# Down projection of sixteen experts: column groups, scatter and layout of the weights

## The chip, the core and the metric

The kernel runs on one core of a Trainium2 chip. Its engines work side by side, each through its own list of instructions in order: TensorE (PE; its weight loads are listed apart as PEld), VectorE (DVE), ScalarE (ACT), GpSimd (POOL) and SyncE (SP), which here issues the loads of weights. Sixteen DMA engines move the data. The metric is the time of one execution on the device in microseconds (us), median over runs.

## The reference

Two transformer blocks run over 256 tokens of 1024 columns, in fp32. The first has a mixer (linear attention beside differential attention) and a layer of sixteen experts; the second has latent and windowed attention, each followed by an MLP. The change lies in the experts, where each expert takes the 32 tokens with the highest affinity to it:

```python
aff = softmax(h @ w_router); top_aff, top_idx = top_k(aff.T, 32)      # 16 experts, 32 tokens each
xin = h[top_idx]
g, u = xin @ w_gate, xin @ w_up                                       # [1024, 1024] per expert
y = (silu(g) * u) @ w_down * top_aff                                  # w_down [1024 (F), 1024 (D)]
f = zeros(256, 1024).at[top_idx].add(y)
x = x + gt2 * rmsnorm(f, norm_post_ffn)
```

## The kernel before

**Weights.** All large weights stream through a ring of slots of 1 MB (128 partitions of 8 KB) in the order of their use, listed in `queue_loads` (L1644 on). A slot is loaded again when the work on it is done: `ring.done` issues the next load of the list into the slot just freed, on SP's queue (L99). Several pools of slots exist. In the experts there are rings A (3 slots), B (4), C (5), D (3) and X (5, no longer refilled after expert 1); C and D are no longer refilled after expert 13 (L1792). An expert has twelve slots: four of gate and four of up alternating, then four of down. The two layers' memory weights (two slots each) come in after the experts 5 and 7.

**An expert** (`experts`, L996 on) goes through these steps.

- Gate and up (L1022): 32 tokens need 32 columns of the array only, so each quarter of F has its own group of 32 columns; four matmuls of 256 columns run for each of the eight parts of the contraction. An fp32 matmul is two instructions in the trace.
- The scatter matrix S (L1029 to L1032), [4 x 32 slots, 256 tokens]: the 32 slots four times over on the 128 partitions, with the affinity at the token's place.
- silu(g) * u on ScalarE and VectorE (L1034 to L1038), two transposes (L1041) and a copy `hs` (L1043), by which F lies on the partitions.
- Down (L1051): the slot g holds the rows 256 g to 256 g + 255 of `w_down`, in two parts c of 128 rows; row p of a part lies on partition p. The slot feeds the group g of 32 columns only, for both halves n of the columns of D, which go to two banks `pd[n]`. So a group holds the sum over a quarter of F.
- Evacuation (L1066): `pd[0]` by VectorE, `pd[1]` by ScalarE, into `yp` [128, 1024].
- Scatter (L1068): `acc[T][n] += S^T yp` for two tiles T of tokens and two halves n; the contraction over 128 partitions sums the four groups too. `acc` holds four banks over all experts.

The last expert takes its down weights by quarters of the columns instead (L1055 to L1068, the line of the matmuls is L1062), each slot on all four groups, so that a quarter is evacuated and scattered as soon as it is done.

`side[e]` adds other work behind some experts: the gathering of later experts' inputs behind experts 1 and 2, the norm, keys and values of the memory behind 4 to 9, the second gate behind 11. On TensorE some of it lies between the down matmuls of an expert.

After the last expert, `rms_add` (L246) takes for each of the four `acc[T][n]` a sum of squares on ScalarE (L251) and a product with the gate on VectorE (L252), then the factor per token and the sum into x (L259). The second block begins with transposes of x (L1156).

Of the kernel before, what the change touches and what calls it, by code (L numbers as in the profile page):

```python
# [19 lines left out]
P = 128  # L20
D = 1024
# [4 lines left out]
# ---------------------------------------------------------------- constants of shapes alone  # L26
# [49 lines left out]
class Ring:  # L76
    """Slots of [P, 2048] that the weights stream through, in the order in which they are used."""
# [8 lines left out]
    def want(self, key, src, part=0, parts=1):  # L86
        """src [P, k, n] in DRAM, or the part-th of the parts of it"""
        self.queue.append((key, src, part, parts))

    def load(self, pool):  # L90
        """the next of the queue into a slot; then the later parts of what has its slot"""
        self.n += 1
        t = pool.tile([P, 2048], F32, tag="ring", name=f"ring{self.n}")
        while True:
            key, src, part, parts = self.queue.pop(0)
# [27 lines left out]
class K:  # L123
# [14 lines left out]
    def isqrt(self, pool, a, m=1, out=None, part=P):  # L138
        """a ** -0.5 for a [P, m] tile: exp(-ln(a) / 2), then a step of Newton's."""
# [14 lines left out]
    def rstd(self, pool, ss, n, m=1, out=None, part=P):  # L154
        """(ss / n + eps) ** -0.5 for a [P, m] tile of sums of squares."""
        a = pool.tile([part, m], F32, tag="rs_a", bufs=2, name=self.nm("rs_a"))
        self.nc.vector.tensor_scalar(a, ss, 1.0 / n, EPS, op0=ALU.mult, op1=ALU.add)
        return self.isqrt(pool, a, m, out, part)

    def split(self, raw, n, view=lambda v: v, eng=None):  # L160
        """the two parts of [P, n] weights, n at most 512"""
# [7 lines left out]
    def three(self, out, a, w, a_st, first, last, asl, wsl):  # L169
        """out += a_hi w_hi + a_hi w_lo + a_lo w_hi, with a or w stationary."""  # L170
# [6 lines left out]
def ada_col(k, t, ps, pool, dst, tag, tbufs):  # L177
    """512 columns of the modulation for silu(c), silu(c_ctx): those of d = 4 p + j at dst [p, 2, j]."""
    nc = k.nc
# [15 lines left out]
def ada_quarter(k, q, ps, pool, dst):  # L195
    """256 columns of scale and of shift for silu(c), silu(c_ctx): those of d = 256 q + 2 p + j at dst [p, 2, 2, j]."""
    nc = k.nc
    pa = ps.tile([P, 2, P], F32, tag="o", bufs=1, name=k.nm("pa"))
    for i in range(2):
        rv = k.ring.get("ada4", q, i).rearrange("p k (n j) -> p k j n", j=2)  # L200
        # columns of the array by j and by half of the contraction
# [15 lines left out]
def ada_sum(k, t, h, pool, dst):  # L217
    """half the contraction of 512 columns of the modulation for silu(c), still to be summed over the partitions."""
# [9 lines left out]
def second_gate(k, st, pool, ps):  # L228
    """the gate of the second residual, in the place of the sums that it is made of"""
# [16 lines left out]
def rms_add(k, pool, acc, x, G, tmp, junk, order):  # L246
    """x += G * rmsnorm(acc), of 1024 columns; order: that in which the halves come"""
# [14 lines left out]
def first_mixer(k, perm, st, ringA):  # L262
    """x += gt1 * rmsnorm(mixer(x)); leaves the modulations of what follows in st."""
# [33 lines left out]
    # ------------------------------------------------ loads  # L297
# [31 lines left out]
    # ------------------------------------------------ silu(c), silu(c_ctx)  # L329
# [14 lines left out]
    # ------------------------------------------------ normalised, modulated inputs, transposed and split  # L344
# [17 lines left out]
    def quarter(q):  # L362
        """the rows of h @ W's contraction d = 256 q + ..."""
# [20 lines left out]
    def project(seg, tks, hks, pts):  # L384
        """a part of the contraction of one segment of the input projection."""
# [30 lines left out]
    # what is needed to the end, and what the linear attention alone needs  # L416
# [4 lines left out]
    # ------------------------------------------------ constants  # L421
# [14 lines left out]
    def constants(d):  # L436
        """what the linear attention needs in direction d."""
# [8 lines left out]
    # ------------------------------------------------ lower bound  # L446
# [17 lines left out]
    def gates(d, pts):  # L464
        """k = 1 - f and log f in two parts."""
# [24 lines left out]
    def decayed(d, tk, more=()):  # L490
        """k * exp(sum of the log f that follow within the tile, and all of those of `more`)."""
# [10 lines left out]
    def state(pairs):  # L502
        """sum of k^T v over token tiles, per head."""
# [9 lines left out]
    def transposed(dst, src, scale=1.0):  # L513
        """dst [P, 4, P] (or two [P, 2, P]) <- per head transposes of src [P, 512]."""
# [11 lines left out]
    # ------------------------------------------------ values, gates and states of the linear attention  # L526
# [3 lines left out]
    for seg, d in ((3, 0), (4, 1)):  # L530
# [8 lines left out]
        # what the first tile of the direction adds to the state that enters its second  # L539
# [11 lines left out]
    # ------------------------------------------------ linear attention  # L551
# [8 lines left out]
    def powers(u):  # L560
        """exp of sums of log f over spans of tokens, times k and q."""
# [24 lines left out]
    def scores(u):  # L586
        """scores [s, r] within a tile."""
# [48 lines left out]
    # ------------------------------------------------ lambda  # L636
# [15 lines left out]
    # ------------------------------------------------ keys of the differential attention  # L652
# [26 lines left out]
    # ------------------------------------------------ gate of the linear attention's output  # L679
# [15 lines left out]
    # ------------------------------------------------ values and queries of the differential attention  # L695
    # ------------------------------------------------ modulation ahead of the experts, gates of the residuals
# [5 lines left out]
    # the router on the rows before their norm: A2 * Wr, and B2 Wr on every partition  # L702
# [27 lines left out]
    # ------------------------------------------------ gates of the residuals  # L730
# [14 lines left out]
    # ------------------------------------------------ differential attention  # L745
# [4 lines left out]
    def weights(u):  # L750
# [10 lines left out]
        # p0 - lam (den0 / den1) p1, to be divided by den0  # L761
# [21 lines left out]
    # ------------------------------------------------ output projection and residual  # L783
    acc = []

    def turned_cat(c, tp):
        """128 columns of cat, transposed and split."""
# [1034 lines left out]
```

## Time and profile before

| | us |
|---|---|
| median of 3 runs | 1429.52 |
| lowest and highest | 1427.45, 1433.12 |
| span of the profiled execution | 1424.5 |

For the profiled execution the span alone is given, from its first to its last instruction; it lies 5.0 us under the median of the runs. The experts' matmuls begin at about 382 us and the second block at about 858 us of the span. The page divides the span into 40 slices and gives the bytes moved in each. The view of stretches gives for any stretch the busy time of each engine, the clock granted to TensorE (1.00 is 2.4 GHz, 0.50 is 1.2 GHz) and the rate of the transfers. The chain of waits goes back from the last instruction to what released each; the timeline lists the instructions in order of time, alike neighbours merged.

### The profile page before, as it was taken

The numbers are of one execution on the slowest core, as the hardware profiler recorded it, in microseconds if no ns is written. First come the engines' busy times: TensorE is split into PE (matmuls) and PEld (weight loads), VectorE is DVE, ScalarE is ACT, GpSimd is POOL, SyncE is SP. The second block draws the span as 40 slices with busy tenths as digits, with TensorE's granted clock in tenths as the row PEclk, the third lists the DMA queues.
The fourth block names the chain that finished last, engine by engine and source line by source line (L and its number), as shares of the span: only waits on it lengthen the run. The fifth ranks groups of instructions, "written<-read, shape, count | busy, mean of one in ns | idle before, by whom it ended". The sixth has DMA issues, their size and how long they took to land.

```text
span 1424.5 us, 22187 instructions
## 1 busy us (share of the span) xinstructions
PE 1309.2 (92%) x8719; PEld 927.4 (65%) x8719; DVE 711.3 (50%) x1595; ACT 574.1 (40%) x1304; POOL 147.3 (10%) x161
## 2 busy tenths in 40 slices
PE   5999988988699988999999879999999999999997
PEld 4776677855335433444433338889989888898996
DVE  5566788667511111111101017857566576766655
ACT  3466223486211112111110126646555555565554
POOL 1112443074000000000000002200000002000000
PEclk9999999999699999999999989999999999999999
DMA  9723513785799999999999994435655643356540
GB/s 317 257 89 136 190 34 83 248 317 178 312 415 391 368 417 416 395 413 397 416 415 416 418 393 147 150 95 178 199 186 199 195 140 90 107 194 201 180 161 30
DMA packets 103236, 352.10 MB, mean 247 GB/s; under 512 B 7041, under 2 KB 20002, under 8 KB 86236
## 3 DMA queue, kind: packets, MB, share of 16 engines
q1 hardware_dynamic: 101024, 346.86, 65.4%
q0 software_dynamic: 1344, 3.21, 0.9%
q8 instruction: 68, 1.11, 0.3%
q10 hardware_dynamic: 764, 0.63, 0.1%
q14 instruction: 36, 0.29, 0.1%
HBM read 349.62 MB, written 1.05 MB: 246 GB/s over the span
## 4 chain that ended last, share of the span: by engine, by line
PE 76%; DVE 11%; ACT 5%; issue 5%; DMA 3%; POOL 0%; ACTq 0%; DVEq 0%; POOLq 0%
PE pd L1051 12%; PE mpu L173 11%; PE macc L173 11%; PE pj L173 5%; PE eacc L1068 4%; PE pg L1022 4%; PE oacc L173 3%; PE pu L1022 3%; DVE wlo L166 2%; PE pk L173 2%; PE spu L173 2%; PE gp L935 2%; PE ob L1200 2%; DMA ring<-in_w_gate_dram 1%; ACT whi L165 1%
## 5 line engine op out<-in xcount | busy, mean ns | idle before, releaser
L166 DVE TENSOR_TENSOR wlo<-ring,whi 128x512 fp32r<-128x512 f32 (+3 forms) x459 | 306.6, 674 | 243.6 <-ACT whi L165 242.3
L165 ACT CAST whi<-ring 128x512 fp32r<-128x512 f32 (+3 forms) x465 | 273.0, 595 | 286.3 <-DVE wlo L166 127.4
L1051 PE MATMUL pd<-ring,hs 128*32 128x512 f32 x480 | 172.4, 631 | 6.9 <-ACT hs L1043 6.9
L173 PE MATMUL mpu<-h,whi 128*128 128x256 f32 x1024 | 177.7, 277 | 0.4 <-ACT whi L165 0.4
L173 PE MATMUL macc<-whi,a 128*128 128x512 f32 x512 | 160.9, 391 | 0.0
L173 PEld LDWEIGHTS mpu<-h,whi 128*128 128x128 f32 x1024 | 155.5, 188 | 1.3 <-ACT whi L165 0.8
L173 PE MATMUL mpu<-h,wlo 128*128 128x256 f32 x512 | 141.0, 277 | 0.6 <-DVE wlo L166 0.6
L173 PE MATMUL pj<-whi,hT 128*128 128x512 f32 x416 | 136.5, 401 | 0.0
L1051 PEld LDWEIGHTS pd<-ring,hs 128*32 128x32 f32 x480 | 41.2, 115 | 118.4 <-issue 106.4
L173 PEld LDWEIGHTS macc<-whi,a 128*128 128x128 f32 x512 | 96.2, 188 | 19.7
L173 PE MATMUL macc<-wlo,a 128*128 128x512 f32 x256 | 100.4, 392 | 0.0
L173 PEld LDWEIGHTS mpu<-h,wlo 128*128 128x128 f32 x512 | 96.2, 188 | 1.5 <-DVE wlo L166 1.0
L173 PEld LDWEIGHTS pj<-whi,hT 128*128 128x128 f32 x416 | 77.6, 188 | 17.1 <-ACT whi L165 0.2
L173 PE MATMUL pj<-wlo,hT 128*128 128x512 f32 x208 | 83.5, 402 | 0.0
L1022 PE MATMUL pg<-ring,xin 128*32 128x256 f32 x1024 | 71.8, 386 | 1.9 <-DMA ring<-in_w_gate_dram 1.9
L1022 PE MATMUL pu<-ring,xin 128*32 128x256 f32 x1024 | 69.9, 385 | 1.5 <-DMA ring<-in_w_up_dram 1.5
L1068 PE MATMUL eacc<-yp,S 128*128 128x512 f32 (+1 forms) x136 | 60.8, 588 | 9.5 <-ACT yp L1066 8.4
L1066 DVE COPY yp<-pd 128x512 f32<-128x512 f32 (+1 forms) x17 | 11.2, 660 | 107.1 <-PE pd L1051 103.8
L173 PEld LDWEIGHTS macc<-wlo,a 128*128 128x128 f32 x256 | 48.1, 188 | 10.6
L1068 PEld LDWEIGHTS eacc<-yp,S 128*128 128x128 f32 x136 | 24.9, 194 | 45.3 <-issue 21.9
L1066 ACT COPY yp<-pd 128x512 f32<-128x512 f32 (+1 forms) x17 | 9.5, 560 | 109.2 <-PE pd L1051 99.9
L575 POOL TENSOR_TENSOR kl<-ex,kT 128x512 f32<-128x512 f32 (+1 forms) x32 | 45.5, 1435 | 67.3 <-ACT ex L572 67.3
(492 smaller groups left out, 2066.8 us busy)
## 6 DMA issues: line engine op xcount, KB each, us to landing
ring<-in_w_gate_dram SPq DMA_DIRECT2D x64, 1024.0 KB, 9.0
ring<-in_w_up_dram SPq DMA_DIRECT2D x64, 1024.0 KB, 12.3
ring<-in_w_down_dram SPq DMA_DIRECT2D x64, 1024.0 KB, 13.6
ring<-in_mlp_w_up_dram SPq DMA_DIRECT2D x32, 1024.0 KB, 5.8
ring<-in_mlp_w_down_dram SPq DMA_DIRECT2D x32, 1024.0 KB, 5.0
ring<-in_w_ada_dram SPq DMA_DIRECT2D x24, 1024.0 KB, 7.8
ring<-in_w_in_dram SPq DMA_DIRECT2D x32, 512.0 KB, 4.9
ring<-in_w_o_dram SPq DMA_DIRECT2D x8, 1024.0 KB, 5.1
```

The source lines that it names most:

```text
L165: nc.scalar.copy(view(hi[:, :n]), raw)
L166: (eng or nc.vector).tensor_tensor(view(lo[:, :n]), raw, view(fl(hi[:, :n])), op=ALU.subtract)
L173: self.nc.tensor.matmul(out, lhsT=av if a_st else wv, rhs=wv if a_st else av, start=first and i == 0, stop=last and i == 2)
L575: nc.gpsimd.tensor_tensor(kl[half_][:, 0:n], ex[:, 0:n], kT[d][:, T, None, h, :].to_broadcast([P, n, P]), op=ALU.mult)
L935: nc.tensor.matmul(gp, lhsT=x[:, T, :].rearrange("p (h n k) -> p h k n", h=2, k=4)[:, h, kk, :], rhs=oh[:, T].rearrange("p e s -> p (e s)" ...
L1022: nc.tensor.matmul(pt[32 * j:32 * j + 32, :], lhsT=xin[:, hk, es_], rhs=w[:, kk, 256 * j:256 * j + 256], start=hk == 0, stop=hk == 7)
L1051: nc.tensor.matmul(pd[n][32 * g:32 * g + 32, :], lhsT=hs[:, c * P + 32 * g:c * P + 32 * g + 32], rhs=wd[:, c, n * 512:n * 512 + 512], star ...
L1066: (nc.scalar.copy if q % 2 else nc.vector.tensor_copy)(yq, pd[n][:, ns])
L1068: nc.tensor.matmul(acc[T][n][:, ns], lhsT=S[:, T * P:T * P + P], rhs=yq, start=e == 0, stop=e == 15 and q % 2 == 1)
L1200: nc.tensor.matmul(self.ob[:, T, n, :], lhsT=pt[:, b * P:b * P + P], rhs=val(c), start=i == 0, stop=i == len(blocks[T]) - 1)
```

## The change

The down weights of all experts, the last included, are loaded with two neighbouring rows to a partition, so a partition's part of a slot is 8 KB in one piece. The transposes take every second column of silu(g) * u to match. A slot g now feeds all four groups: group 2 n + c takes the part c of the slot for the half n of D's columns, and all four slots accumulate there, in one bank. The two halves n lie on 64 partitions each, VectorE evacuates the first, ScalarE the second, into a `yp` of [128, 512] (two buffers instead of one), and the scatter contracts over these 64 partitions, which also sums the two parts c. The last expert's own way is gone; its scatter ends with all four banks, and `rms_add` takes them in another order. (The diff also takes out comments.)

```diff
-            nc.tensor.transpose(ht[:, c * P:c * P + P], ge[:, c * P:c * P + P], ident)
+            nc.tensor.transpose(ht[:, c * P:c * P + P], ge.rearrange("p (n c) -> p c n", c=2)[:, c, :], ident)
...
-        yp = small("yp", (P, D), bufs=1)
-        pd = [wk("pd") for _ in range(2)]
-        if e < 15:
-            for g in range(4):
-                wd = ring.get("down", e, g)
-                for c in range(2):
-                    for n in range(2):
-                        nc.tensor.matmul(pd[n][32 * g:32 * g + 32, :], lhsT=hs[:, c * P + 32 * g:c * P + 32 * g + 32],
-                                         rhs=wd[:, c, n * 512:n * 512 + 512], start=c == 0, stop=c == 1)
-                ring.done("down", e, g)
...
-            yq = yp[:, q * w:q * w + w]
-            (nc.scalar.copy if q % 2 else nc.vector.tensor_copy)(yq, pd[n][:, ns])
-            for T in range(2):
-                nc.tensor.matmul(acc[T][n][:, ns], lhsT=S[:, T * P:T * P + P], rhs=yq, start=e == 0, stop=e == 15 and q % 2 == 1)
+        pd = wk("pd")
+        for g in range(4):
+            wd = ring.get("down", e, g)
+            for c in range(2):
+                for n in range(2):
+                    j = 2 * n + c
+                    nc.tensor.matmul(pd[32 * j:32 * j + 32, :], lhsT=hs[:, c * P + 32 * g:c * P + 32 * g + 32],
+                                     rhs=wd[:, c, n * 512:n * 512 + 512], start=g == 0, stop=g == 3)
+            ring.done("down", e, g)
+        yp = small("yp", (P, 512))
+        for n, copy in enumerate((nc.vector.tensor_copy, nc.scalar.copy)):
+            copy(yp[64 * n:64 * n + 64, :], pd[64 * n:64 * n + 64, :])
+        for T in range(2):
+            for n in range(2):
+                ns = slice(64 * n, 64 * n + 64)
+                nc.tensor.matmul(acc[T][n], lhsT=S[ns, T * P:T * P + P], rhs=yp[ns, :], start=e == 0, stop=e == 15)
...
-    k.rms_add(pool, acc, x, st["G2"], [tmp[:, T] for T in range(2)], lambda: wk("raj"), ((0, 0), (1, 0), (0, 1), (1, 1)))
+    k.rms_add(pool, acc, x, st["G2"], [tmp[:, T] for T in range(2)], lambda: wk("raj"), ((0, 0), (0, 1), (1, 0), (1, 1)))
...
-        dv = A["w_down"][0, e].rearrange("(g k p) n -> p g k n", g=4, k=2)
-        if e == 15:
-            dv = A["w_down"][0, e].rearrange("(m p) (q n) -> p q m n", p=P, q=4)
+        dv = A["w_down"][0, e].rearrange("(g p k) n -> p g k n", g=4, k=2)
```

## Rows read from the trace of the kernel before

**Rows 1.** Page, part 2: GB/s of the transfers in 40 equal slices.

```profile
GB/s 317 257 89 136 190 34 83 248 317 178 312 415 391 368 417 416 395 413 397 416 415 416 418 393 147 150 95 178 199 186 199 195 140 90 107 194 201 180 161 30
```

**Rows 2.** Stretches with pauses of the transfers; the first line names columns.

```profile
core 0: us, PE busy (x) PEld busy (x) DVE busy (x) ACT busy (x) POOL busy (x), PEclk, DMA share, GB/s
444.00:482.00 38.00, 34.87 (x330) 19.77 (x322) 5.18 (x13) 6.21 (x15) 0.58 (x1) 1.00 0.89 346
592.00:597.00 5.00, 5.00 (x69) 2.32 (x71) 0.60 (x2) 0.37 (x1) 0.00 (x0) 1.00 0.78 270
661.00:666.00 5.00, 5.00 (x90) 2.82 (x86) 0.60 (x2) 0.37 (x1) 0.00 (x0) 1.00 0.78 277
```

**Rows 3.** The same view, same columns, for stretches without pauses.

```profile
722.00:740.00 18.00, 16.02 (x130) 6.17 (x127) 2.13 (x5) 2.54 (x6) 0.00 (x0) 1.00 1.01 420
711.00:721.00 10.00, 9.32 (x44) 3.16 (x44) 0.69 (x1) 0.58 (x1) 0.00 (x0) 1.00 1.02 407
742.00:752.00 10.00, 10.00 (x23) 3.19 (x22) 1.29 (x2) 1.17 (x2) 0.00 (x0) 1.00 1.03 414
833.00:844.00 11.00, 7.99 (x62) 3.19 (x65) 1.27 (x3) 1.59 (x4) 0.00 (x0) 0.59 1.08 349
844.00:845.00 1.00, 1.00 (x16) 0.35 (x8) 0.00 (x0) 0.00 (x0) 0.00 (x0) 0.50 1.13 401
```

**Rows 4.** DMA view, its line of packets for 722:740, 742:752 and 833:844.

```profile
DMA packets 1043, 7.55 MB, mean 420 GB/s; under 512 B 112, under 2 KB 112, under 8 KB 132
DMA packets 1043, 4.14 MB, mean 414 GB/s; under 512 B 64, under 2 KB 64, under 8 KB 1012
DMA packets 3709, 3.84 MB, mean 349 GB/s; under 512 B 59, under 2 KB 3694, under 8 KB 3698
```

**Rows 5.** Timeline, SP's queue at the first pause: start us, us, what.

```profile
432.51 0.33 SPq L99 DMA_DIRECT2D ring<-in_w_up_dram  x1
447.21 2.96 SPq L99 DMA_DIRECT2D ring<-in_w_down_dram  x4
```

**Rows 6.** Chain of waits, pieces in order of time: start us, us, what.

```profile
443.56 1.00 PE pg L1022 x16
...
473.12 1.00 PE pg L1022 x16
...
660.81 1.00 PE pg L1022 x16
...
695.43 1.00 PE pg L1022 x16
...
705.41 10.48 PE pd L1051 x32
716.55 3.70 PE eacc L1068 x8
720.25 1.00 PE pg L1022 x16
```

**Rows 7.** Timeline of TensorE in the first mixer, same columns.

```profile
338.58 1.13 PE L758 MATMUL sc<-kTda,qTda 64*128 64x512 f32 x4
...
341.38 1.10 PE L741 MATMUL pg<-G,onesr 128*128 128x512 f32 x2 [0.20 <-ACT ax L760]
```

**Rows 8.** Timeline of several engines, from expert 14's evacuation on.

```profile
820.00 0.69 DVE L1066 COPY yp<-pd 128x512 f32<-128x512 f32 x1 [8.99 <-PE pd L1051]
...
835.42 1.93 PE L1022 MATMUL pu<-ring,xin 128*32 128x256 f32 x16 [1.45 <-DMA ring<-in_w_up_dram]
...
849.64 1.07 PE L1062 MATMUL pd<-ring,hs 128*32 128x256 f32 x16
...
851.94 0.58 ACT L251 ACTIVATE raj<-eacc 128x512 f32<-128x512 f32 x1 [0.79 <-PE eacc L1068]
...
852.66 1.29 DVE L252 TENSOR_TENSOR xin<-eacc,G 128x512 f32<-128x512 f32 x2 [3.54 <-ACT raj L251]
...
857.14 2.74 DVE L259 SCALAR_TENSOR_TENSOR x<-xin,rs_r,x 128x512 f32<-128x512 f32 x4
```

More of the change, by code (lines that the diff above doesn't have):

```diff
@@ L1055, in experts @@
-        for q in range(2 if e < 15 else 4):
-            n, w = (q, 512) if e < 15 else (q // 2, 256)
-            ns = slice(0, 512) if e < 15 else slice(256 * (q % 2), 256 * (q % 2) + 256)
-            if e == 15:
-                wd = ring.get("down", e, q)
-                for c in range(2):
-                    for g in range(4):
-                        nc.tensor.matmul(pd[n][32 * g:32 * g + 32, ns], lhsT=hs[:, c * P + 32 * g:c * P + 32 * g + 32],
-                                         rhs=wd[:, 2 * g + c, :], start=c == 0, stop=c == 1)
-                ring.done("down", e, q)
-            yq = yp[:, q * w:q * w + w]
-            (nc.scalar.copy if q % 2 else nc.vector.tensor_copy)(yq, pd[n][:, ns])
-            for T in range(2):
-                nc.tensor.matmul(acc[T][n][:, ns], lhsT=S[:, T * P:T * P + P], rhs=yq, start=e == 0, stop=e == 15 and q % 2 == 1)
+        pd = wk("pd")
@@ L1690, in queue_loads @@
                 ring.want(("up", e, h, i), uv[:, h, 2 * i:2 * i + 2])
-        dv = A["w_down"][0, e].rearrange("(g k p) n -> p g k n", g=4, k=2)
-        if e == 15:
-            dv = A["w_down"][0, e].rearrange("(m p) (q n) -> p q m n", p=P, q=4)
+        dv = A["w_down"][0, e].rearrange("(g p k) n -> p g k n", g=4, k=2)
         for g in range(4):
```

## The prediction

> **What bounds the kernel now.** I read the page's row of memory traffic first. Forty slices of 35.6 us: from the twelfth to the twenty-fourth, which is the experts' stage, they move 368 to 418 GB/s, most of them over 410, and nowhere else does the kernel do so for long [rows 1]. So in the experts the transfer of the weights sets the pace, however busy TensorE looks. Next I cut the stage into stretches by its own joints, to see where the transfers pause. They do so in three places, 444 to 482, 592 to 597 and 661 to 666 us [rows 2], and in each TensorE is busy nearly throughout: there the ring of weight slots was full and waited for TensorE. The queue of loads shows how: after 432.51 us nothing is issued until 447.21 [rows 5], 3.65 us after expert 2's first gate matmuls began at 443.56 [rows 6]; its first slots are the first to be refilled. The chain of waits gives TensorE's pace: an expert lasts 24.8 us without side work (695.43 to 720.25) and 34.6 us with the memory's keys or values between (660.81 to 695.43) [rows 6], against twelve slots of 1.049 MB, 30.0 us at 420 GB/s. TensorE is ahead in some experts and behind in others, but the stage ends on the transfers: the last expert waits for its last up weights [rows 8]. A microsecond taken from TensorE thus counts only inside the three pauses; a microsecond taken from the transfers, or from what follows the last of them, counts fully.
>
> **The change part by part.**
>
> **Down matmuls.** Now a slot feeds one group of 32 columns, so its matmuls mostly queue behind each other: 10.48 us for an expert [rows 6]. Afterwards a slot's four matmuls go to four groups. The last expert is already fed so: 16 instructions of 256 columns over four groups take 1.07 us at full clock, about 0.2 us of it the ends [rows 8]. An expert's down has 32 instructions of 512 columns, four times that: 4 x 0.87 + 0.2 = 3.7 us. The saving is 6.8 us an expert; at half clock (1.93 us for the same 16, rows 8) it would be 7.1 us long and save 3.4.
>
> **Scatter.** It keeps its eight instructions of 512 columns, now on 64 rows each, two row groups in turn, into different banks. Before, 3.70 us [rows 6]. The nearest row is the first mixer's pair of scores on 64 rows each: four instructions in 1.13 us, as long as two instructions on 128 rows (1.10) [rows 7], so a pair costs what one did. Two pairs: 2.0 us, 1.7 saved. If they didn't overlap: 3.7, nothing saved.
>
> **Small parts.** The two evacuations, each of half the partitions of one bank, still take 0.69 us [rows 8] side by side; at worst, one after the other, 0.6 more. The transposes read with a stride of two; the bank freed earlier delays nobody. All of this is hidden by the transfers, except behind the last slot. The order of loads, and which slot frees which, is as before.
>
> **What TensorE's 8.5 us are worth.** Experts now need 16.3 us, 26.1 with memory columns, and expert 2 with its gathering 21.1 instead of 29.6 (443.56 to 473.12) [rows 6], all below 30.0. The first pause would need expert 2 to start as late as 443.56; it starts two savings, 17 us, earlier, so the refills come at about 430, before the queue has run dry. The third and fourth pauses (592, 661) come after further experts with the same gain. What is late next is the transfer itself. Each pause is worth its length times the share that it lacks of 416 GB/s: 38 x (1 - 346/416) = 6.4; 5 x (1 - 270/416) = 1.75; 5 x (1 - 277/416) = 1.67 [rows 2]. **Together 9.8 us**; none of it if the ring stays the limit.
>
> **Two rows to a partition.** Gate and up come in packets of 8 KB, down in packets of 4 KB, the last expert's down, cut by columns, in 1 KB [rows 4]. Stretches of the first sort move 420 GB/s; of the second 407, in one case 414; of the third 349 [rows 3]. A slot costs 2.50, 2.58 (2.53) and 3.00 us. Experts 1 to 14 have 56 down slots in the bound stretch (those of expert 0 come before it): 56 x 0.08 = **4.5 us**, 2.0 by the 414. The last four: 4 x 0.5 = **2.0 us**.
>
> The row shows 3% between 4 KB and 8 KB packets. The Trainium skill (DMA: Bandwidth & Descriptors, Why small descriptors are slow) has a fixed cost of some 3 cycles beside 32 bytes a cycle, which makes it 1.2%, an estimate from that page; and 8% between 1 KB and 8 KB where the row shows 20; the 56 slots would then give 1.6 us, the last four 0.8, and the whole come out 4.1 us later than I say. The measured stretches decide for me.
>
> **Tail.** Here the change costs. Before, the last slot was a quarter of the columns, and the halves done earlier had their squares behind them. The last 1 KB packets end at about 844.1 us [rows 3]; a slot is seen by TensorE some 2.5 us after its bytes (the rate falls to 349 at 833, where down begins, and the last up matmuls start at 835.42 [rows 3, 8]), so the last slot was there at 846.6, and the last product of the norm is done at 852.66 + 1.29 = 853.95: 7.3 us. After: down of one slot 1.9 at half clock, evacuation 0.75, first scatter pair 2.0, second 1.7 later, then the second pair's squares and products, 2.0 from the first square's start to the last product [rows 8]: 8.4 us. At full clock it is 6.3, VectorE's four products of 0.65 us being the limit; without overlap of the row groups, at half clock, 11.8. I take 8.4, **1.1 us lost** (bounds -1.0 and +4.5), since TensorE waits for transfers then, as at 833 to 844 us, where the granted clock was 0.59 [rows 3].
>
> Sum: 9.8 + 4.5 + 2.0 - 1.1 = **15.2 us**. The profiled execution spans 1424.5 us, and 1409.3 is what its successor should span; the median of the runs shown is 1429.5, 5.0 above the span, and with the same 5.0 the time is 1414.3, say 1414. The second block, which begins with the finished rows, moves as a whole; its first weights queue right behind the last down slots before and after.
>
> **Rivals.**
>
> *The packet size is not what makes down slow* (it shares the queue with other traffic then): 9.8 + 2.0 - 1.1 = 10.7 us, 1419. For it, the one stretch at 414; against it, the 1 KB row, in order with the other two.
>
> *The pauses stay*, because the ring's own rule holds slots (a ring of five is closed after expert 1, the memory's weights hold two): 4.5 + 2.0 - 1.1 = 5.4, 1424. Against it stands 17 us of margin at the first pause.
>
> *The clock, slower than before.* With TensorE waiting for transfers in every expert, its clock could stay at 1.2 GHz. At 833 to 844 us it waited and was granted 0.59; at 722 to 740, busy 16 of 18 us, 1.00 [rows 3]. An expert with memory columns takes 26.1 us after the change; counted as if all of it were TensorE's, 52.2, or 22 us over the transfers in each of the four experts that have them: 89 us, minus the 15: 1503. It decides from a mean clock below 26.1 / 30.0 = 0.87 in those experts; plain ones (16.3 us) need 0.54. Against it: when TensorE falls behind it has no waits left, and every stretch above without waits shows 1.00. So a brief loss is likelier, hidden by the ring.
>
> The Trainium skill (TensorE: Matmul & The Clock Gate, HAM oscillation) says that matmul bursts shorter than the waits for DMA between them find the clock halved each time. By that rule alone the time would be that 1503; the stretch at 833 agrees, but no run here shows it for an expert with memory columns.
>
> *The change doesn't do what it says*: the four groups run one after the other, 32 instructions of 0.43 us (two in 1.10 us with their ends, rows 7), 13.7 us instead of 10.5. With 1.7 from the scatter an expert loses 1.5 us; over the eight with gathering or memory columns the pauses grow by 12, and with the gain from packets it is 12 - 5.4: 1436. Against it, the last expert's 1.07 us [rows 8].
>
> **How the numbers follow.** Forecast 0.66, packets 0.12, pauses 0.09, clock 0.05, groups 0.03, others 0.05. The range: from 1408 (15.2 plus the tail's 2.1 at full clock, plus the runs' own spread) to 1424 (the pauses stay; it takes in 1419 and the unpaired scatter's 1418). What a measurement can tell from no change is 0.5%, 7.1 us, so the line lies at 1422.4: faster 0.79 (forecast, packets, some of the others), same 0.13, slower 0.08.
>
> **What would show it.** The row of traffic without its dips in the thirteen slices, 415 or more; down stretches at 420 like gate and up; down matmuls of 3.7 us an expert and a scatter near 2.0; TensorE idle before gate and up, released by DMA, in most experts; granted clock below 1.00 in plain experts; the residual's update (before, at 857.14, rows 8) at about 842. I am wrong if pauses remain, if down stays at 407, if the clock makes experts with memory columns longer than 30 us, or if the tail behind the last slot is over 10 us.

## The result, and the profile after

| | before | after |
|---|---|---|
| median, us | 1429.32 | 1412.21 |
| lowest and highest, us | 1427.45, 1433.12 | 1411.39, 1415.58 |
| span of the profiled execution, us | 1424.5 | 1411.2 |
| first gate matmul to the residual's update, us | 475.2 | 460.8 |

Four runs of each; the ratio is 0.988, 95% interval 0.986 to 0.990: by the ratio 16.6 us less, where 15.2 were forecast. The changed kernel was timed once more in the study, with 1412.37 us beside 1427.24 (ratio 0.989, interval 0.988 to 0.991). The last row of the table compares the stage itself, from the first gate matmul of expert 0 (381.91 before, 382.30 after) to the first update of x (857.14 in [rows 8], 843.09 after): 14.4 us less. I use this length below, since the runs differ ahead of the stage: its first gate matmul begins between 379.5 and 384.7 us in the executions below, with the same code before it.

The page of the changed kernel, part 2: granted clock in tenths and GB/s in 40 slices, now of 35.3 us. It answers to [rows 1].

```profile
PEclk9999999998699978988777869999999999999999
GB/s 312 267 90 123 206 34 58 254 313 186 295 416 418 419 421 420 419 420 419 420 421 419 421 372 107 180 90 182 186 200 191 207 120 109 108 189 192 185 159 31
```

From the twelfth to the twenty-third slice every value lies between 416 and 421; the dips of [rows 1] to 391, 368, 395 and 397 are gone. In these slices the granted clock is mostly below its full speed, where the kernel before kept it nearly throughout.

The view of stretches, first of the kernel before, then of the changed one; 396 us is after the opening of the stage, 826 just ahead of the last expert's down. The columns stand in the first line.

```profile
core 0: us, PE busy (x) PEld busy (x) DVE busy (x) ACT busy (x) POOL busy (x), PEclk, DMA share, GB/s
396.00:640.00 244.00, 220.82 (x1588) 100.27 (x1588) 37.45 (x98) 42.71 (x109) 1.12 (x2) 0.97 0.99 402
640.00:826.00 186.00, 170.08 (x1190) 68.80 (x1190) 20.06 (x46) 23.21 (x55) 1.00 (x2) 0.96 1.01 413
```

```profile
396.00:640.00 244.00, 190.53 (x1782) 95.84 (x1782) 41.89 (x109) 47.76 (x122) 1.12 (x2) 0.90 1.01 420
640.00:826.00 186.00, 140.65 (x1130) 52.77 (x1122) 16.25 (x37) 20.35 (x48) 1.00 (x2) 0.77 1.01 420
```

Moving the bytes of the first stretch at 420 instead of 402 GB/s saves 244 x (1 - 402/420) = 10.5 us, those of the second 186 x (1 - 413/420) = 3.1. So **13.6 of the 14.4 us** are made before the last expert's down begins. The timelines agree: TensorE begins on the last slot of up weights 453.5 us after the first gate matmul before (835.42, [rows 8]) and 440.4 after (822.66), 13.1 us earlier; 1.3 us come behind it. TensorE is busy 60 us less in these 430 us, and the time of the stage shrank by a quarter of that only.

The groups of instructions by line, before and then after: instructions, then busy us and mean ns of one, then idle time just before them and its releaser.

```profile
L1051 PE MATMUL pd<-ring,hs 128*32 128x512 f32 x480 | 172.4, 631 | 6.9 <-ACT hs L1043 6.9
L1068 PE MATMUL eacc<-yp,S 128*128 128x512 f32 (+1 forms) x136 | 60.8, 588 | 9.5 <-ACT yp L1066 8.4 <-DVE yp L1066 1.1
L1022 PE MATMUL pg<-ring,xin 128*32 128x256 f32 x1024 | 71.8, 386 | 1.9 <-DMA ring<-in_w_gate_dram 1.9
```

```profile
L1052 PE MATMUL pd<-ring,hs 128*32 128x512 f32 x512 | 83.4, 756 | 20.3 <-DMA ring<-in_w_down_dram 12.8 <-ACT hs L1044 7.4
L1061 PE MATMUL eacc<-yp,S 64*128 64x512 f32 x128 | 48.5, 759 | 18.7 <-DVE yp L1057 18.7
L1022 PE MATMUL pg<-ring,xin 128*32 128x256 f32 x1024 | 79.9, 426 | 22.1 <-DMA ring<-in_w_gate_dram 22.1
```

Down's busy time is halved though its mean instruction is longer (756 ns against 631): four groups now work at a time. The longer mean comes with the lower clock; expert 0, at full clock in both kernels, has 592 ns in both. And TensorE has become the one that waits: 22.1 us for gate weights instead of 1.9, 12.8 for down weights instead of none.

Last the tail, from the timeline of the changed kernel; it answers to [rows 8].

```profile
830.13 1.93 PE L1052 MATMUL pd<-ring,hs 128*32 128x512 f32 x8 [0.95 <-DMA ring<-in_w_down_dram]
832.63 1.93 PE L1052 MATMUL pd<-ring,hs 128*32 128x512 f32 x8 [0.57 <-DMA ring<-in_w_down_dram]
834.63 0.68 DVE L1057 COPY yp<-pd 64x512 f32<-64x512 f32 x1 [10.42 <-PE pd L1052]
835.35 0.58 ACT L1057 COPY yp<-pd 64x512 f32<-64x512 f32 x1 [10.16 <-DVE yp L1057]
835.37 4.39 PE L1061 MATMUL eacc<-yp,S 64*128 64x512 f32 x8 [0.81 <-DVE yp L1057]
837.48 0.58 ACT L251 ACTIVATE raj<-eacc 128x512 f32<-128x512 f32 x1 [1.55 <-PE eacc L1061]
...
841.13 0.69 DVE L252 TENSOR_TENSOR xin<-eacc,G 128x512 f32<-128x512 f32 x1 [0.20 <-ACT raj L251]
...
843.09 1.41 DVE L259 SCALAR_TENSOR_TENSOR x<-xin,rs_r,x 128x512 f32<-128x512 f32 x2
843.90 3.94 PE L1149 MATMUL ntp<-ident,x 128*128 128x128 f32 x16 [4.14 <-DVE x L259]
```

The slots arrive 2.5 us apart and TensorE waits for each, at half clock (1.93 us for eight instructions; at full clock 1.06). What the sum had otherwise is ScalarE's copy: it starts at 835.35, when VectorE's is done, and not beside it.

### The profile page after: what moved, and what is told of

Same layout as the page of the kernel before. It is cut to its first block, busy times and chain, and to the rows that moved or that the text cites. A ratio compares the mean times of both kernels' runs of the same rounds, so it can differ in the third digit from the quotient of the medians.

```text
span 1411.2 us, 22092 instructions
## 1 busy us (share of the span) xinstructions
PE 1242.5 (88%) x8679; PEld 902.3 (64%) x8679; DVE 709.2 (50%) x1594; ACT 574.6 (41%) x1303; POOL 147.7 (10%) x161
## 4 chain that ended last, share of the span: by engine, by line
PE 51%; DMA 30%; DVE 9%; issue 5%; ACT 4%; POOL 1%; ACTq 0%; SPq 0%; DVEq 0%; POOLq 0%
PE mpu L173 12%; PE macc L173 11%; DMA ring<-in_w_gate_dram 10%; DMA ring<-in_w_down_dram 10%; DMA ring<-in_w_up_dram 9%; PE pj L173 5%; PE oacc L173 3%; DVE wlo L166 2%; PE spu L173 2%; PE ob L1193 2%; DMA ring<-in_w_mem_kv_dram 1%; ACT whi L165 1%; DVE ql L583 1%; PE ptp L1236 1%; PE pe L568 1%
## 5 line engine op out<-in xcount | busy, mean ns | idle before, releaser
L1022 PE MATMUL pu<-ring,xin 128*32 128x256 f32 x1024 | 79.3, 427 | 26.1 <-DMA ring<-in_w_up_dram 26.1
L1052 PE MATMUL pd<-ring,hs 128*32 128x512 f32 x512 | 83.4, 756 | 20.3 <-DMA ring<-in_w_down_dram 12.8
L1022 PE MATMUL pg<-ring,xin 128*32 128x256 f32 x1024 | 79.9, 426 | 22.1 <-DMA ring<-in_w_gate_dram 22.1
L1022 PEld LDWEIGHTS pu<-ring,xin 128*32 128x32 f32 x1024 | 33.4, 119 | 64.4 <-DMA ring<-in_w_up_dram 43.4
L1022 PEld LDWEIGHTS pg<-ring,xin 128*32 128x32 f32 x1024 | 30.8, 117 | 66.1 <-DMA ring<-in_w_gate_dram 34.1
L1037 DVE TENSOR_TENSOR ge<-ge,pg 128x256 f32<-128x256 f32 x16 | 6.7, 420 | 129.9 <-ACT ge L1036 129.9
L1061 PE MATMUL eacc<-yp,S 64*128 64x512 f32 x128 | 48.5, 759 | 18.7 <-DVE yp L1057 18.7
L1034 ACT ACTIVATE ge<-pg 128x256 f32<-128x256 f32 x16 | 6.1, 383 | 123.3 <-PE pg L1022 123.3
```

Source lines behind the costliest of these rows:

```text
L1022: nc.tensor.matmul(pt[32 * j:32 * j + 32, :], lhsT=xin[:, hk, es_], rhs=w[:, kk, 256 * j:256 * j + 256], start=hk == 0, stop=hk == 7)
L1037: nc.vector.tensor_tensor(ge, ge, pg, op=ALU.mult)
L1052: nc.tensor.matmul(pd[32 * j:32 * j + 32, :], lhsT=hs[:, c * P + 32 * g:c * P + 32 * g + 32], rhs=wd[:, c, n * 512:n * 512 + 512], start=g ...
L1061: nc.tensor.matmul(acc[T][n], lhsT=S[ns, T * P:T * P + P], rhs=yp[ns, :], start=e == 0, stop=e == 15)
```

## The experiments

The theory: the pauses (9.8 us) and the packets (4.5 and 2.0) are two separate gains, and TensorE's speed counts only as far as it ends the pauses. The rivals: packets alone, or TensorE alone, do it all; the pauses stay; the clock takes the gain back. The runs undo or do one part at a time. Ratios are to the kernel before on the same chip. Where two medians stand side by side they can come from different chips, on which the kernel before took 1427.2 to 1429.3 us.

### The packets alone

The kernel before, with the new layout of the down weights (8 KB packets) for the experts 0 to 14 and the strided transposes; the matmuls are as before.

```diff
-            nc.tensor.transpose(ht[:, c * P:c * P + P], ge[:, c * P:c * P + P], ident)
+            gv_ = ge.rearrange("p (n c) -> p c n", c=2)[:, c, :] if e < 15 else ge[:, c * P:c * P + P]
+            nc.tensor.transpose(ht[:, c * P:c * P + P], gv_, ident)
...
-        dv = A["w_down"][0, e].rearrange("(g k p) n -> p g k n", g=4, k=2)
+        dv = A["w_down"][0, e].rearrange("(g p k) n -> p g k n", g=4, k=2)
```

> The kernel before, with one part of the change alone: the experts 0 to 14 load their down weights two rows to a partition (8 KB packets), down matmuls, scatter and the last expert as before. Additive theory: 56 slots of 0.08 us, 4.5 us under the kernel before's 1429.3, 1424.8. Rival, that the two parts need each other: up to the last pause (666 us) TensorE sets the pace, so faster packets only lengthen the pauses, and only the five experts 10 to 14 gain, 20 slots of 0.08 = 1.6 us: 1427.7, with the pauses longer by some 3 us and down stretches at 420 GB/s. If packets don't matter at all: 1429.3 with down stretches at 407. I hold the rival, 1427.7.

Measured: 1429.96 us (1422.74 to 1436.78, ten runs) against 1428.91 (thirteen runs); ratio 1.001, interval 0.999 to 1.003. The profiled execution is the fastest of the ten; its stretches:

```profile
396.00:640.00 244.00, 220.81 (x1576) 100.83 (x1570) 37.47 (x98) 42.46 (x109) 1.13 (x2) 0.97 0.98 403
640.00:826.00 186.00, 170.07 (x1190) 69.58 (x1190) 20.08 (x46) 23.23 (x55) 1.00 (x2) 0.96 1.00 415
470.00:475.00 5.00, 5.00 (x59) 3.66 (x58) 0.64 (x2) 1.02 (x2) 0.00 (x0) 1.00 0.36 125
660.00:665.00 5.00, 5.00 (x81) 2.60 (x82) 0.60 (x2) 0.37 (x1) 0.00 (x0) 1.00 0.69 238
```

TensorE is busy for the same 220.8 and 170.1 us, so up to 640 us the rate rises from 402 to 403 only: what the faster packets bring comes back as deeper pauses (125 GB/s at 470 to 475, where the kernel before, whose stage began 1.0 us later, has 162 at 471 to 476; 238 at 660 to 665 against 277 at 661 to 666 in [rows 2]). Behind the last pause experts 10 to 14, whose down loads are issued from 668 us on, could keep their 20 x 0.08 = 1.6 us. The profiled stage is 3.1 us shorter (472.1), but only 0.8 of that is there when the last slot of up weights is begun (452.75 us after the first gate matmul, against 453.51); the other 2.3 come behind it, where this execution had TensorE at full clock and the kernel before at half (1.07 and 1.93 us for the same sixteen instructions), and are no gain of the packets. The median of ten runs shows nothing. Why this kernel's runs are so wide apart, 14 us, stays open. Taken alone, the packets are worth between 0 and 1 us, not 4.5: **where TensorE sets the pace, a faster transfer only waits longer.**

### The groups alone

The changed kernel with the old layout: 4 KB packets in all sixteen experts, plain transposes.

```diff
-            nc.tensor.transpose(ht[:, c * P:c * P + P], ge.rearrange("p (n c) -> p c n", c=2)[:, c, :], ident)
+            nc.tensor.transpose(ht[:, c * P:c * P + P], ge[:, c * P:c * P + P], ident)
...
-        dv = A["w_down"][0, e].rearrange("(g p k) n -> p g k n", g=4, k=2)
+        dv = A["w_down"][0, e].rearrange("(g k p) n -> p g k n", g=4, k=2)
```

> The changed kernel with one row to a partition again for all sixteen experts (4 KB packets); column groups and scatter as changed. If the packets carry their 0.08 us a slot where the transfers are the bound throughout, 60 slots give 4.8 us over the changed kernel's 1412.2: 1417.0, no pauses, down stretches at 407. If the gain of the change is all from the pauses: 1412.2.

Measured: 1415.05 us (1414.18 to 1416.54), ratio 0.991, interval 0.989 to 0.992. Its stretches:

```profile
396.00:640.00 244.00, 191.74 (x1766) 96.37 (x1761) 41.91 (x109) 47.79 (x121) 1.13 (x2) 0.87 1.02 416
640.00:826.00 186.00, 140.19 (x1112) 51.96 (x1108) 15.42 (x35) 19.31 (x46) 1.00 (x2) 0.75 1.02 416
```

No pauses, and 416 GB/s throughout. Against the kernel before, with packets of the same size in the experts up to 14, the rates rise from 402 and 413 to 416: 244 x (1 - 402/416) + 186 x (1 - 413/416) = 9.6 us, which is what the pauses cost. Groups and scatter were not tried apart. Against the changed kernel, which moves 420, it is 430 x (1 - 416/420) = 4.1 us for the packets, against 4.5 of the sum. The stage is 463.4 us long, 2.6 over the changed kernel's, with a tail that was by chance at full clock and 1.8 us shorter: 4.4, of which 0.8 lie in the stage's opening (376 GB/s against 408 in ten us). The medians say less: 2 to 3 us by the ratios, where 4.8 were expected. So the packets' term is there once TensorE no longer sets the pace. The Trainium skill (DMA: Bandwidth & Descriptors, Why small descriptors are slow) would have 1.6 us here, the estimate from its figures that stands in the prediction; by its rates this run does not agree.

### TensorE's time given back, half and all of it

The changed kernel with extra down matmuls in the experts 0 to 14, at slot 0, into the same bank ahead of the real ones: 16 of them, and 32 (32 shown).

```diff
             wd = ring.get("down", e, g)
+            for i in range(8 if e < 15 and g == 0 else 0):
+                for j in (0, 2, 1, 3):
+                    nc.tensor.matmul(pd[32 * j:32 * j + 32, :], lhsT=hs[:, 32 * j:32 * j + 32], rhs=wd[:, j % 2, 0:512], start=True, stop=True)
```

> The changed kernel with 16 extra down matmuls of 512 columns on the four groups in each of the experts 0 to 14 (their results are overwritten): 3.4 us of TensorE more an expert, half of what the change takes away. Theory (the transfers bind, TensorE has room): 1412.2, within 1 us, no pauses. Rival (TensorE's time counts): 15 x 3.4 = 52 us more, 1464; if it counts in the eight experts with gathering or memory columns alone, 27 more, 1439.

> The changed kernel with 32 extra down matmuls in each of the experts 0 to 14: 6.9 us of TensorE more an expert, which makes down as long as before (10.5 us), while packets and scatter stay changed. Theory: most of the pauses come back, 9.8 us less what the 1.7 us of the scatter spare an expert, and in the experts ahead of a pause the packets' gain goes into it: 1419 to 1425, pauses in the traffic near 450, 475, 590 and 660 us. Rival (the gain came from the packets and the tail, not from TensorE's time): 1412.2 without pauses.

Measured: half 1417.53 us (1410.27 to 1418.14), ratio 0.991, interval 0.988 to 0.994; all 1422.46 (1422.16 to 1422.77), ratio 0.996, interval 0.994 to 0.997. The stretches of the full dose:

```profile
396.00:640.00 244.00, 221.07 (x2194) 103.85 (x2198) 37.52 (x99) 43.11 (x110) 1.13 (x2) 0.97 0.98 404
640.00:826.00 186.00, 162.75 (x1610) 69.28 (x1602) 20.12 (x46) 23.55 (x56) 1.00 (x2) 0.95 1.01 419
405.00:415.00 10.00, 10.00 (x89) 3.63 (x82) 0.68 (x1) 0.58 (x1) 0.00 (x0) 1.00 0.75 286
475.00:480.00 5.00, 5.00 (x87) 3.11 (x90) 0.23 (x1) 0.51 (x1) 0.00 (x0) 1.00 0.55 185
490.00:500.00 10.00, 10.00 (x89) 3.60 (x82) 0.68 (x1) 0.58 (x1) 0.00 (x0) 1.00 0.74 284
```

The 32 extra matmuls bring TensorE's busy time in the first stretch back to 221 us, and pauses with it: 10 x (1 - 286/420) + 5 x (1 - 185/420) + 10 x (1 - 284/420) = 9.2 us. The median is 10.3 us over the changed kernel's, 9 to 10 by the ratios, where the forecast priced the pauses at 9.8. But they are not the same pauses. All lie between 405 and 500 us, and of the four places that were expected only the one near 475 has one; at 590 to 600 and 660 to 665 the rate is 419. The dose gives back 6.9 of the 8.5 us and holds slot 0 of each expert for all of it; how much of the 9.2 comes from the place of the extra matmuls and how much from their time, no run separates. The stretches of the half dose, the third being the place where the full dose first pauses:

```profile
396.00:640.00 244.00, 210.82 (x2029) 103.00 (x2032) 42.30 (x110) 47.91 (x122) 1.13 (x2) 0.94 1.01 419
640.00:826.00 186.00, 142.16 (x1345) 54.15 (x1336) 15.42 (x35) 18.79 (x44) 1.00 (x2) 0.89 1.01 420
405.00:415.00 10.00, 10.00 (x105) 4.14 (x101) 0.68 (x1) 0.58 (x1) 0.00 (x0) 1.00 0.99 401
```

With 16 there are no pauses but a dip worth 10 x (1 - 401/420) = 0.5 us. The stage, 463.2 us, is 2.4 longer than the changed kernel's 460.8, and as long as that of the next experiment, 463.1, which has no extra matmul. So the time does not follow TensorE's work: the first half of the dose costs no more than two executions differ by, the second half costs pauses. The median of the half dose missed what was expected, 1412.2 within 1 us: it is 5.3 over, 2 to 4 by the ratios, and three of the four runs stand near 1417.5. In the profiled one of these 2.1 us of the 4.6 between the two profiled runs lie ahead of the stage (its first gate matmul begins at 384.37, the changed kernel's at 382.30). By the medians alone a small cost of the half dose is not ruled out.

### The scatter, one row group after the other

```diff
-        for T in range(2):
-            for n in range(2):
+        for n in range(2):
+            for T in range(2):
                 ns = slice(64 * n, 64 * n + 64)
```

> The changed kernel with the scatter's four matmuls in another order: both on the row group 0 to 63 first, then both on 64 to 127, so that neighbours share a row group. If row groups overlap only when neighbours differ, a scatter takes 3.7 us at full clock instead of 2.0, hidden in the stage; behind the last slot about 1.5 to 3 us more at half clock, less what the second evacuation hides (0.6): 1413 to 1415. If the row groups don't overlap anyway, or the tail hides it: 1412.2, and the scatter in the trace lasts as long as in the changed kernel.

Measured: 1412.56 us (1411.16 to 1415.61), ratio 0.990, interval 0.989 to 0.992. The lines view gives 48.8 us for its scatter, 48.5 in the changed kernel. At full clock one expert's takes 2.59 us in both where it starts on VectorE's copy, and 1.99 in both in experts 1 and 2, where both copies were done before it started; in the tail it is 4.39 in both. The order of the four products is worth nothing here; why, no run shows. What holds the other scatters above the 2.0 us of the forecast is the second copy, as the two-bank runs below show.

### The last expert by columns

The changed kernel, with the last expert as in the kernel before: 1 KB packets, a slot for each quarter of the columns, the scatter over 128 partitions.

```diff
+        if e == 15:
+            dv = A["w_down"][0, e].rearrange("(m p) (q n) -> p q m n", p=P, q=4)
...
+                for c in range(2):
+                    for g in range(4):
+                        nc.tensor.matmul(pd[n][32 * g:32 * g + 32, ns], lhsT=hs[:, c * P + 32 * g:c * P + 32 * g + 32],
+                                         rhs=wd[:, 2 * g + c, :], start=c == 0, stop=c == 1)
...
```

> The changed kernel with the last expert as before (down by quarters of the columns in 1 KB packets, two banks, scatter over 128 partitions, the order of the norm's halves as before). My sum has 2.0 us lost on the packets and 1.1 won in the tail: 0.9 over the changed kernel, 1413.1. Rival, that the tail as changed costs much more than 1.1: as far as 1409.

Measured: 1414.34 us (1412.16 to 1417.68), ratio 0.991, interval 0.990 to 0.993; a stage of 461.3 us against 460.8. Between 826 and 836 us its transfers move 374 GB/s, those of the changed kernel at the same point (824 to 834) 418: 1.1 us. Its tail is shorter by 3.0 us (7.5 from the start of the last slot's matmuls to the update, against 10.5), but its last slot is a quarter of the columns that comes later. The two ways come out within what the profiles can tell; by the medians rows are 2 us better, with intervals that overlap.

### Two banks, and TensorE kept busy

Three kernels for the tail. One gives the two halves of the last expert's result a bank each:

```diff
-        pd = wk("pd")
+        pds = [wk("pd") for _ in range(2)] if e == 15 else [wk("pd")] * 2
...
-                    nc.tensor.matmul(pd[32 * j:32 * j + 32, :], lhsT=hs[:, c * P + 32 * g:c * P + 32 * g + 32],
+                    nc.tensor.matmul(pds[n][32 * j:32 * j + 32, :], lhsT=hs[:, c * P + 32 * g:c * P + 32 * g + 32],
...
-            copy(yp[64 * n:64 * n + 64, :], pd[64 * n:64 * n + 64, :])
+            copy(yp[64 * n:64 * n + 64, :], pds[n][64 * n:64 * n + 64, :])
```

The second makes the last scatter matrix ahead of gate and up and adds matmuls whose result nobody reads (`warm`) behind each slot of the last expert and behind its scatter; it also writes all squares of the norm to one bank. The third does both.

```diff
+                for j in range(12 if e == 15 else 0):
+                    jj = j % 4
+                    nc.tensor.matmul(warm[32 * jj:32 * jj + 32, 0:256], lhsT=xin[:, 0, es_], rhs=w[:, 1, 256 * jj:256 * jj + 256], start=True, stop=True)
...
+            for j in range((6 if g < 3 else 0) if e == 15 else 0):
+                jj = j % 4
+                nc.tensor.matmul(warm[32 * jj:32 * jj + 32, :], lhsT=hs[:, 0:32], rhs=wd[:, 1, 0:512], start=True, stop=True)
...
```

> The changed kernel with the last expert's two halves in two banks, so that VectorE and ScalarE evacuate them at the same time. In the changed kernel's trace ScalarE's evacuation begins when VectorE's ends (835.35 after 834.63 + 0.68), and the four scatter matmuls take 4.39 us. If sharing the bank is the reason, the second evacuation moves up by 0.7 us and the tail shortens by 0.3 to 0.7 us: 1411.7, which the times can't tell from 1412.2 but the trace can. If it isn't, the two still run one after the other.

> The changed kernel with TensorE kept busy in the last expert: twelve extra matmuls of 256 columns behind each gate and up slot, six of 512 behind each of the first three down slots, four behind the last, and four of 512 on 128 rows behind the scatter, all into a bank that nobody reads; the norm's squares use one bank. If the tail is long because the clock is at 1.2 GHz there, it is granted 2.4 and the last down (1.93 us) takes 1.1, the scatter (4.39) 2.7, the tail 2 to 2.5 us less: 1410. If the clock doesn't follow or the tail hangs on VectorE and ScalarE: 1412.2 or more, by up to 2 for the extra work.

> The changed kernel with both edits of the tail: the last expert's halves of the result in two banks, and TensorE kept busy in the last expert by matmuls whose result is not used, with the last scatter matrix made earlier. If the tail behind the last slot is worth what the timelines say, the x update begins 8.1 us after the last down slot's matmuls begin (8.8 with the busy TensorE alone, 10.5 in the changed kernel) and the transposes of the second block take 1.4 us a half instead of 3.9 together, so that the second block's first matmul comes some 3 us earlier behind the last slot and the median is about 1409, 0.2% under the changed kernel's. The rival: the opening of the stage, where the transfers start after a gap that differs from run to run by some microseconds, covers it, and the median is within 2 us of the changed kernel's.

> The changed kernel itself, beside the one with both edits of the tail, so that the two share a chip: median 1412.2 by its runs so far (1411.4 to 1415.6); its x update 10.5 us after the last down slot's matmuls begin if TensorE is at the half clock there, 8.7 if by chance at the full one.

Measured: two banks 1411.61 us (1410.46 to 1413.05); kept busy 1415.89 (1411.24 to 1418.2); both 1413.15 (1411.32 to 1413.9), beside the changed kernel again, 1412.37 (1410.48 to 1414.3). None beats it; the 1410 and 1409 that the second and third were to reach if the clock was what made the tail long were missed. The timeline of the kernel with two banks:

```profile
830.42 1.93 PE L1052 MATMUL pd<-ring,hs 128*32 128x512 f32 x8 [0.57 <-DMA ring<-in_w_down_dram]
832.40 0.68 DVE L1057 COPY yp<-pd 64x512 f32<-64x512 f32 x1 [10.40 <-PE pd L1052]
832.45 0.58 ACT L1057 COPY yp<-pd 64x512 f32<-64x512 f32 x1 [9.47 <-PE pd L1052]
833.08 3.45 PE L1061 MATMUL eacc<-yp,S 64*128 64x512 f32 x8 [0.73 <-ACT yp L1057]
```

Both copies now wait for the matmuls alone and run side by side, and the scatter at half clock takes 3.45 us instead of 4.39. So it was the shared bank that put them one behind the other. The last product of the norm ends 8.2 us after the last slot's matmuls begin (838.63), against 9.2 in the changed kernel; the update comes 10.0 us after them, 0.5 less than there; that is too little for the median. With both edits, the scatter takes the 2.0 us of the forecast:

```profile
837.81 0.68 DVE L1072 COPY yp<-pd 64x512 f32<-64x512 f32 x1 [10.54 <-PE pd L1062]
837.86 0.58 ACT L1072 COPY yp<-pd 64x512 f32<-64x512 f32 x1 [8.94 <-PE pd L1062]
838.49 2.04 PE L1076 MATMUL eacc<-yp,S 64*128 64x512 f32 x8 [0.30 <-ACT yp L1072]
...
844.29 1.41 DVE L259 SCALAR_TENSOR_TENSOR x<-xin,rs_r,x 128x512 f32<-128x512 f32 x2
```

Its last slot's matmuls begin at 835.87, without a wait for the transfer, and the update follows 8.4 us later; in the changed kernel beside it they begin at 832.70, and the update follows 9.5 us later (842.21; TensorE was by chance back at full clock for the scatter, 2.59 us). Counted from the first gate matmul, the last slot is worked on after 453.8 us and after 451.2. So TensorE was late by 2.5 us, more than the 1.1 that the full clock and the two banks gave back. It was late before down: the scatter of expert 14 ran at half clock there (4.39 us from 805.76), and from then on the chain shows matmuls, real and added, without a wait for weights, so that the delay was never made up. In the kernel kept busy alone, where that scatter took 2.59 us, TensorE still met the last up slot as it came (a wait of 0.16 us), and its last slot was worked on after 452.4 us. How much of the delay is the added matmuls, which left no room to catch up, and how much the clock of that one execution, was not tried.

## Why the prediction was right, step by step

**What bounds the stage.** Right, and shown from both sides: the groups alone end the pauses at the old packet size; with 32 extra matmuls an expert there are pauses again and the median rises by 10.3 us; with 16 there are none.

**The pauses, 9.8 us.** All are gone as forecast. Their price is measured by the groups alone, 9.6 us by the rates. The 9.2 us of the full dose lie in other places and are close to 9.8 in part by luck.

**The packets, 4.5 us.** The run with 4 KB packets shows 4.1 by the rates. Down slots now move as gate and up do; the 3% between the two packet sizes in [rows 3] was the right price, and the rival that something else had slowed down's transfers falls. But the prediction added the terms as if each stood by itself. They don't: without TensorE's gain the packets bring 0 to 1 us.

**Down, 3.7 us an expert.** The chain has 3.64 for expert 0's 32 instructions at 400.15 us, at full clock. The rival of groups that run one after the other (13.7 us) falls.

**Scatter, 2.0 us.** 1.99 at full clock where both copies are done when it starts, 2.59 where it starts on the first. The row groups overlap as [rows 7] said, 2.04 in the tail with two banks; the other 0.55 is ScalarE's copy, which waits for VectorE's as long as both read one bank. The prediction had that as its worst case (0.6 more) and took the better one.

**Tail, 1.1 us lost.** From the start of the last slot's matmuls to the end of the last product I had 8.4 us, at half clock. It was 832.63 to 841.82, 9.2: the 0.8 more is again the copies' order, for with two banks, at half clock too, it is 8.2. Behind it something was gained that the prediction hadn't looked at: the update starts 1.3 us after the last product (843.09 - 841.82), before it was 3.2 (857.14 - 853.95, [rows 8]), since the banks now come token tile by token tile, and the first tile's factor is on its way while the second's products run. The second half of the update follows later in return (845.06), so that the second block's first projection begins 14.2 us earlier, not 14.4 (847.50 against 861.34, each less its first gate matmul).

**The sum.** Before the last expert's down, 13.6 us of 14.3 forecast by the rates; the last expert and the tail together 14.4 - 13.6 = 0.8, of 2.0 - 1.1 = 0.9 (13.1 and 1.3 by the timelines). That the second number is so close is luck, since the prediction had its path wrong. It let the last slot's transfer, estimated at 846.6, end the wait in the kernel before. The chain of that kernel has no transfer behind the last up slot:

```profile
826.26 9.11 DMA ring<-in_w_up_dram
...
835.42 1.98 PE pu L1022 x16
...
839.05 1.98 PE pd L1062 x16
...
841.53 2.07 PE eacc L1068 x4
843.60 1.86 PE pd L1062 x16
...
847.03 1.05 PE pd L1062 x16
...
849.71 1.04 PE pd L1062 x16
```

Matmuls, at half clock up to 845 us, copies and scatters follow each other there, and the last slot is worked on 3 us after the estimated 846.6. In the execution of the packets alone, at full clock, three of these four slots are waited for (1.02, 0.19 and 0.41 us), and 19.4 us pass from the last up slot's matmuls to the update, where the kernel before has 21.7 and the changed one 20.4. So what the last expert gained or lost lies within what the clock does there, and the 2.0 us for its packets and the 1.1 lost are not shown each by itself.

**The clock.** It did fall, to a mean of 0.77 between 640 and 826 us, for TensorE waits for weights now; the transfers stayed at 420 GB/s all the same. The rival asked for a mean below 0.87 in experts with memory columns, and the clock was there or a little under it in stretches of 35 us:

```profile
550.00:585.00 35.00, 29.39 (x256) 16.24 (x255) 6.70 (x16) 7.95 (x20) 0.00 (x0) 0.88 1.01 419
585.00:620.00 35.00, 26.89 (x229) 13.09 (x226) 5.29 (x14) 6.22 (x16) 0.00 (x0) 0.85 1.01 420
620.00:655.00 35.00, 29.03 (x244) 15.64 (x242) 5.87 (x14) 6.77 (x17) 0.00 (x0) 0.80 1.01 419
```

Even so TensorE is idle for 6 to 8 of the 35 us. The rival's price had the clock at its lower level through the whole expert (52.2 us); it fell for parts only, and the ring of slots covered these. The Trainium skill (TensorE: Matmul & The Clock Gate, HAM oscillation) holds that the clock halves when bursts are shorter than the waits between them: that it falls, this trace agrees (1.07 us of matmuls at 812.34 between waits of 1.40 and 1.42, then 1.93 us for as many at 814.83); not each time, for the bursts at 574.25 and 576.75, behind waits of 1.41 and 1.42, still take 1.07. That it costs time, these stretches don't show; behind the last slot it does, 4.39 us for a scatter against 2.59.

**Span and median.** I took the 5.0 us between the profiled span and the median as a constant. In every run that has both, the time is 1.7 or 1.8 us over its own span (1412.96 and 1411.2 for the changed kernel); the other 3.2 was the place of that one execution, which is not among the runs listed and lies under all of them. The span came 1.9 us later than forecast, the median 1.8 earlier; the nearness of 1414 to 1412 is in part these two errors.

## What to carry to other kernels

Where a ring of slots joins a transfer and an engine, look for the stretches in which the transfers pause: here faster compute was worth those pauses and nothing more, and faster transfers next to nothing as long as there were pauses behind them, so the two gains must be priced in that order and not each by itself. A dose of extra work, half and all of what was saved, shows how much slack is left, but where it is put decides which pauses come back. And price the tail by its chain of single instructions, once you have looked in the chain before whether a transfer ends it at all: it was the only part where the sum had to be mended.

## What was not expected of the hardware

- Two engines that read different partitions of one result bank ran one after the other (834.63 and 835.35); from two banks they ran together (832.40 and 832.45). In the trace the second waits for the first one's copy, so it is a wait in the program; whether the engines could share the bank, no run shows.
- At half clock and behind the same waits, TensorE's clock came back between down and scatter in one execution (1.93 and 2.59 us) and not in another (1.93 and 4.39). The scatter of one kernel thus differs by 1.8 us from run to run, and its tail by 0.9 (10.5 and 9.5 us from the last slot's matmuls to the update).
- The stage opens with a gap that the change doesn't touch: from 380 to 384 us nothing is transferred, before and after, while the slots are full and expert 0 has not yet freed one; the ten us that begin 4 us after the first gate matmul show between 364 and 408 GB/s, 1.0 us from one execution to another. That is as much as most edits of the tail are worth.
